# A decoder block with 16 experts: the second pair's gate products moved, three engines in a written order, two small moves in attention

## Chip, cores and metric

The kernel runs on one NeuronCore of one Trainium2 chip. The metric is the device time of one execution in microseconds (us), lower is better; 451.19 us is the median of three runs before the change. The engines are named as in the profile: PE (TensorE, matrix products), DVE (VectorE), ACT (ScalarE), POOL (GpSimd), and SP, which here only issues DMAs.

## What is computed

One block for 256 tokens of 1024 features in float32: two token mixers in parallel, then a mixture of experts. Cut to what matters:

```python
h = rms_norm(x, norm_mix_g)
(f_q, f_k, f_v, f_f, n_q, k_c, v_c, k_s, v_s, k_w, v_w, n_g, g_a, g_b) = split_cols(h @ w_in)
# forgetting attention, 8 heads of 64
out_a = from_heads(fox_attention(rms_norm(f_q), rms_norm(f_k), f_v, log_f)) @ w_fox_up
# sparse attention, 8 query heads over 2 key heads: compressed, selected and window keys
kc = rms_norm(compress_blocks(k_c, cmp_k_w1, cmp_k_w2, cmp_k_pos), nsa_k_g)
vc = compress_blocks(v_c, cmp_v_w1, cmp_v_w2, cmp_v_pos)
out_b = from_heads(nsa_attention(qb, kc, vc, ks_, vs_, kw_, vw_, gates)) @ w_nsa_up
x = x + (sigmoid(g_a) * out_a + sigmoid(g_b) * out_b) @ w_out
# mixture of experts: best of 4 groups, two best of its 4 experts, combine weights w
t = rms_norm(x, norm_ffn_g)
hid = silu(einsum('td,edf->etf', t, w_gate)) * einsum('td,edf->etf', t, w_up)
hid = hid * combine.T[:, :, None]
x = x + einsum('etf,efd->td', hid, w_down)
```

There are 16 experts with a hidden width of 512, so each has 6 MB of weights, 96 MB in all.

## The kernel before

**Attention.** Weight matrices of the mixers are read in pieces of two times 512 columns by 128 rows (`raw`). `hi` makes a rounded copy `wH` on ACT (L173), `lo` the remainder `wL` on DVE (L179); three products per chunk (L199 to L201) then use the high and low parts of weights and activations. The pieces go through a line in which `load`, `hi`, `lo` and `go` (the products of half a piece) run each some pieces apart. `half_a` calls `go`, `lo`, `load` and then the functions it was given; `half_b` calls `go`, `hi` and the functions. All of this is a written order for every engine. Between the pieces stand small jobs: `k_scaled` (L753, two DVE operations) multiplies the keys by their inverse norms into `kdup`, which the PE transposes in `kk_turn` (L730). In a loop over 13 steps n attention units follow: their scores, exponentials, scaling of the scores (`sc`, L579), transposes (L587) and products with the values. A list of background jobs is taken from by `spot`. Three of them are `g_turn`, `c_in` and `c_root`: `c_in` puts the compressed keys and values into one PSUM bank and squares the keys on ACT (L817), `c_root` computes the inverse root on DVE in some ten short operations (from L834) and then reads that bank twice more, for the normalised keys `kcn` (L836) and for `vblk` (L837), the values laid out by head. The bank is one of two with the name `tp`, which go round.

**Experts.** Tokens are routed, and each expert has 64 slots. Experts are taken in pairs, one on each half of the PE's columns, so one product of a pair is two matmuls of 64 columns by 512. Eight pairs follow each other: seven in `expert_pair`, the eighth in `last_pair`. For pair `pr` the PE does `proj` with the gate weights, `proj` with the up weights (each 8 k steps with a matmul per expert, which are 32 rows of the trace, L1347), `scatter` of the previous pair's result to the tokens (L1357, L1358), four transposes of `hid` (L1408) and `down` (L1373). DVE computes `hid` (L1399, written `gh`) from `silu` of the gate product (ACT, L1393 or L1397), and the combine weight of each slot, `csl`; ACT copies the transposes back (L1409). `parts` splits the down product into a high part (ACT, L1361) and a low part (DVE, L1362). `ready` makes the one-hot rows of a pair on DVE (L1007), `slots` turns them into `csl` (PE L1326, DVE L1329 to L1331), and `rows` transposes them for the scatter (PE L1338, DVE L1340); all go through `tp` banks. They are called in the fourth k step of a `proj`: those of pair 0 in its own up products, those of pair 1 in its own gate products (there together with the `rows` of pair 0), all later ones in the up products of the pair before. In odd pairs, between transposes and down products, `gather` collects the tokens of the next two pairs (PE L1317, DVE L1318). After pairs 2 and 4 the residual is added to two accumulators (L1430).

**What sets the order.** In this loop the order of the PE alone is the written one; DVE and ACT are ordered by the scheduler. Expert weights come in tiles of 1 MB, twelve per pair (gate, up, down of two experts, two halves each), issued by SP in that order (L113, at the end L107) into a ring of slots. A load waits until the last matmul that reads the tile before it in its slot has run.

Of the kernel before, what the change touches and what calls it, by code (L numbers as in the profile page):

```python
# [8 lines left out]
F32 = mybir.dt.float32  # L9
# [3 lines left out]
AF = mybir.ActivationFunctionType  # L13
# [17 lines left out]
def block_kernel(ctx, tc, a, out, dbg=None):  # L31
# [608 lines left out]
    with tc.manual_schedule():  # L640
# [128 lines left out]
        half_a(k_scaled)  # L769
# [32 lines left out]
        pw = {}  # L802
# [8 lines left out]
        def c_in():  # L811
            p = pw[0] = bank([128, 512], "tp")
            for f in range(2):
                T.matmul(p[0:32, 0:64], hT[:, f, 0:32], w2[:, 0, f], start=(f == 0), stop=(f == 1))
            for f in range(2):
                T.matmul(p[:, 64:128], hTv[:, f].rearrange("p g r n -> p (g r n)"), w2[:, 1, f], start=(f == 0), stop=(f == 1))
            A.activation(ks_, p[0:32, 0:64], AF.Square, accum_out=kcst[:, 0:1])  # L817

# [12 lines left out]
        ks_ = wk.tile([32, 64], F32, name="kcs", bufs=1)  # L831

        def c_root():
            V.tensor_scalar(kcst[:, 0:1], kcst[:, 0:1], 1.0 / 64, EPS, op0=ALU.mult, op1=ALU.add)  # L834
            rsqrt(kcst[:, 1:2], kcst[:, 0:1], 1, "kc")
            V.tensor_scalar(kcn, pw[0][0:32, None, 0:64].to_broadcast([32, 2, 64]), kcst[:, 1:2], None, op0=ALU.mult)  # L836
            V.tensor_tensor(vblk, pw[0][:, None, 64:128].to_broadcast([128, 8, 64]), hm[:, :, None].to_broadcast([128, 8, 64]), op=ALU.mult)  # L837
# [483 lines left out]
    def slots(pr, Sb):  # L1321

        p = bank([128, 9], "tp")
        for i, cc in enumerate((2 * pr, 2 * pr + 1, 16)):
            for t in range(2):
                T.matmul(p[:, 3 * i:3 * i + 3], Sb[:, t], cb3[:, t, cc], start=(t == 0), stop=(t == 1))  # L1326
        c = wk.tile([128, 3], F32, name="csl")
        j6 = wk.tile([128, 6], F32, name="j6")
        V.tensor_tensor_reduce(j6, p[:, 0:6], half.rearrange("p a b -> p (a b)"), 1.0, 0.0, ALU.mult, ALU.add, c[:, 0:1])  # L1329
        V.tensor_reduce(c[:, 1:2], p[:, 6:9], axis=AX.X, op=ALU.add)  # L1330
        V.tensor_tensor(c[:, 2:3], c[:, 0:1], c[:, 1:2], op=ALU.mult)  # L1331
        return c
# [10 lines left out]
    def proj(w0, w1, xg, o, between=()):  # L1343
        p = bank([128, 512], "z")
        for k in range(8):
# [3 lines left out]
            if k == 3:  # L1349
                for f in between:  # L1350
                    f()
# [34 lines left out]

    def expert_pair(pr, pend):
        xg, o = xgs[pr // 2], pr % 2 * 128
        if pr:
            pg = proj(tiles[2 * pr, 0], tiles[2 * pr + 1, 0], xg, o, pre0)  # L1390
            pre0.clear()
            c, Sb, ST = pre.pop()
            A.activation(sg, pg, AF.Silu, scale=c[:, 1:2])  # L1393
        pu = proj(tiles[2 * pr, 1], tiles[2 * pr + 1, 1], xg, o, [lambda: pre.append(ready(pr + (pr > 0))())])
        if pr == 0:
            c, Sb, ST = pre.pop()
            A.activation(sg, pg0, AF.Silu, scale=c[:, 1:2])  # L1397
# [8 lines left out]
        p = bank([128, 4, 128], "tp")  # L1406
        for f in range(4):
            T.transpose(p[:, f], hid[:, f * 128:f * 128 + 128], ident)  # L1408
        A.activation(hdT, p, AF.Copy)  # L1409
        if pend and pr % 2 == 0:  # L1410
            scatter(*pend, 512, 512)
        if pr % 2 == 1:
            xgs[pr // 2 + 1] = gather(pr // 2 + 1)
        y = rt.tile([128, 2, D], F32R, name="y", tag="yy")
# [16 lines left out]
        if pr == 0:  # L1431
# [3 lines left out]
            pre0.extend([lambda: got.append(rows(Sb)), lambda: pre.append(ready(1)())])  # L1435
# [72 lines left out]
    with tc.manual_schedule(engines={mybir.EngineType.PE}):  # L1508
        pre, pre0 = [], []
        for pr in range(7):  # L1510
            pend = expert_pair(pr, pend)
# [77 lines left out]
```

## Time and profile before

| | |
|---|---|
| runs | 453.54, 451.19, 451.06 us (median 451.19) |
| profiled execution | 451.66 us, of which the span of the trace is 449.7 us |
| PE busy | 430.3 us, 96% |
| DVE, ACT, POOL busy | 214.7, 167.0, 10.5 us |
| granted PE clock, mean | 0.992 |
| DMA | 136.10 MB, mean 303 GB/s |

The profile is of one execution. Times of the trace count from the start of the span. A row of the timeline gives the start, the length, the engine, the line and the instruction (written <- read, the shape, a count); the bracket at its end is the engine's idle time ahead of it and what ended that. A row with a count stands for that many instructions of one kind, one after another. The list of waits sums such idle time by the instruction that waited and the one that ended the wait.

### The profile page before, as it was taken

What the parts mean: (1) busy time and instruction counts of PE and PEld (TensorE: products, weight loads), DVE (VectorE), ACT (ScalarE), POOL (GpSimd) and SP (SyncE); (2) the same over time, 40 slices, a digit from 0 to 9 for tenths busy, and PEclk for the clock granted to TensorE, in tenths of its full rate; (3) what the DMA queues carried; (4) which work ended last, traced back from release to release, by engine and by line L of the source; (5) the groups of instructions that cost most, each with busy time, mean ns of one, the idle gap of its engine ahead of it and who ended that gap; (6) DMA issues with size and microseconds to landing.
All of it is one profiled execution on the core that took longest, in us unless ns stands there. A gap on an engine that the chain in (4) does not pass through costs nothing.

```text
span 449.7 us, 6356 instructions
## 1 busy us (share of the span) xinstructions
PE 430.3 (96%) x2370; PEld 258.9 (58%) x2370; DVE 214.7 (48%) x611; ACT 167.0 (37%) x343; POOL 10.5 (2%) x25
## 2 busy tenths in 40 slices
PE   7998999999999999999999899989999999999994
PEld 4895766767777777878952336333363335433443
DVE  5869776797856565576654224133130512201012
ACT  4786563957767665534732100101011010101011
POOL 8000000000000000000000000000000000000000
PEclk8999999999999999999999999999999999999998
DMA  8699643656763439999889999799999999999922
GB/s 285 131 366 303 216 138 95 222 183 214 254 206 94 129 109 351 408 408 374 352 310 335 351 391 422 280 422 421 420 420 418 420 420 418 422 418 416 391 78 98
DMA packets 41425, 136.10 MB, mean 303 GB/s; under 512 B 7296, under 2 KB 12976, under 8 KB 30384
## 3 DMA queue, kind: packets, MB, share of 16 engines
q1 hardware_dynamic: 41248, 135.54, 80.3%
q8 instruction: 20, 0.33, 0.3%
q10 hardware_dynamic: 144, 0.13, 0.1%
q14 instruction: 13, 0.11, 0.1%
HBM read 134.61 MB, written 1.05 MB: 302 GB/s over the span
## 4 chain that ended last, share of the span: by engine, by line


## 5 line engine op out<-in xcount | busy, mean ns | idle before, releaser
L1347 PE MATMUL z<-m,xg 128*64 128x512 f32 x432 | 100.5, 595 | 0.0
L179 DVE TENSOR_TENSOR wL<-raw,wH 128x1024 fp32r<-128x1024 f32 x48 | 58.4, 1220 | 12.2 <-ACT wH L173 12.0
L173 ACT ACTIVATE wH<-raw 128x1024 fp32r<-128x1024 f32 x48 | 50.5, 1056 | 36.8 <-PE z L201 21.5
L1347 PEld LDWEIGHTS z<-m,xg 128*64 128x64 f32 x432 | 31.5, 137 | 56.5 <-issue 54.6
L199 PE MATMUL z<-wH,hH 128*128 128x512 f32 x128 | 54.4, 425 | 0.0
L200 PE MATMUL z<-wL,hH 128*128 128x512 f32 x128 | 50.4, 393 | 0.0
L201 PE MATMUL z<-wH,hL 128*128 128x512 f32 x128 | 50.3, 393 | 0.0
L1373 PE MATMUL tp<-m,gh 128*64 128x512 f32 (+1 forms) x208 | 49.5, 580 | 0.7 <-ACT gh L1409 0.7
L1373 PEld LDWEIGHTS tp<-m,gh 128*64 128x64 f32 x208 | 15.8, 137 | 28.8 <-issue 25.7
L199 PEld LDWEIGHTS z<-wH,hH 128*128 128x128 f32 x128 | 24.1, 188 | 11.4 <-issue 7.1
L1361 ACT ACTIVATE y<-tp 128x512 fp32r<-128x512 f32 (+1 forms) x15 | 8.6, 583 | 56.7 <-PE tp L1373 56.6
L1340 DVE CAST ST<-tp 128x256 fp32r<-128x256 bf16 x8 | 3.4, 423 | 54.7 <-PE tp L1338 54.7
L1362 DVE TENSOR_TENSOR y<-tp,y 128x512 fp32r<-128x512 f32 (+1 forms) x15 | 10.0, 673 | 36.7 <-ACT y L1361 36.7
L201 PEld LDWEIGHTS z<-wH,hL 128*128 128x128 f32 x128 | 24.1, 188 | 5.5
L1409 ACT ACTIVATE gh<-tp 128x512 f32<-128x512 f32 x7 | 4.2, 598 | 59.6 <-PE tp L1408 59.6
L200 PEld LDWEIGHTS z<-wL,hH 128*128 128x128 f32 x128 | 24.2, 189 | 3.7
L570 ACT ACTIVATE sc<-sc,mx 128x128 f32<-128x128 f32 (+1 forms) x48 | 21.2, 445 | 1.7 <-DVE mx L564 1.4
L1393 ACT ACTIVATE gh<-z,csl 128x512 f32<-128x512 f32 x6 | 4.1, 688 | 39.2 <-PE z L1347 39.2
L1399 DVE SCALAR_TENSOR_TENSOR gh<-gh,csl,z 128x512 f32<-128x512 f32 x7 | 7.9, 1128 | 20.8 <-PE z L1347 15.1
L579 DVE TENSOR_SCALAR sc<-sc,sm 128x128 f32<-128x128 f32 (+1 forms) x48 | 12.1, 316 | 0.4
L1317 PE MATMUL tp<-one,xH 128*128 128x256 f32 x48 | 12.3, 297 | 0.0
L587 PE MATMUL tp<-ident,sc 128*128 128x128 f32 x72 | 10.5, 278 | 1.8 <-DVE vblk L837 1.0
(423 smaller groups left out, 701.5 us busy)
## 6 DMA issues: line engine op xcount, KB each, us to landing
m<-in_w_gate SPq DMA_DIRECT2D x29, 1024.0 KB, 17.2
m<-in_w_up SPq DMA_DIRECT2D x28, 1024.0 KB, 11.5
m<-in_w_down SPq DMA_DIRECT2D x22, 1024.0 KB, 12.5
raw<-in_w_in SPq DMA_DIRECT2D x36, 512.0 KB, 4.6
m<-in_w_down SPq DMA_DIRECT2D x10, 512.0 KB, 9.4
raw<-in_w_out SPq DMA_DIRECT2D x8, 512.0 KB, 10.3
m<-in_cmp_k_w SPq DMA_DIRECT2D x8, 256.0 KB, 8.5
m<-in_cmp_v_w SPq DMA_DIRECT2D x8, 256.0 KB, 4.8
```

The lines of the kernel that those rows point to most:

```text
L173: A.activation(P["H"], P["raw"], AF.Copy)
L179: (eng or V).tensor_tensor(P["L"], P["raw"], P["H"].bitcast(F32), op=ALU.subtract)
L199: T.matmul(p[t], lH[k // 4][:, k % 4, ts], P["H"][:, k - k0], start=(k == 0), stop=False)
L200: T.matmul(p[t], lH[k // 4][:, k % 4, ts], P["L"][:, k - k0], start=False, stop=False)
L201: T.matmul(p[t], lL[k // 4][:, k % 4, ts], P["H"][:, k - k0], start=False, stop=(k == K - 1))
L570: A.activation(sc, sc, AF.Exp, scale=-1.0, bias=u["mx"][:, i, t:t + 1], accum_out=u["sm"][:, i, t:t + 1])
L579: V.tensor_scalar(sc, sc, u["sm"][:, i, t:t + 1], None, op0=ALU.mult)
L587: T.transpose(p[:, 128 * j:128 * j + 128], u["sc"][i][:, 128 * j:128 * j + 128], ident)
L1317: T.matmul(p[:, j], X[t][:, cs], Sr[:, t], start=(i == 0), stop=(i == 3))
L1347: T.matmul(p[64 * i:64 * i + 64], xg[:, k, o + 64 * i:o + 64 * i + 64], w[k // 4][:, k % 4], start=(k == 0), stop=(k == 7), tile_position= ...
L1362: V.tensor_tensor(yHL[:, 1, c0:c0 + n], p[:, 0:n], yHL[:, 0, c0:c0 + n].bitcast(F32), op=ALU.subtract)
L1373: T.matmul(p[64 * i:64 * i + 64, 0:n], hdT[:, f, 64 * i:64 * i + 64], w, start=(f == 0), stop=(f == 3), tile_position=(0, 64 * i))
```

## The change

Four edits. (1) `k_scaled` is issued ahead of the low part of its `half_a`. (2) `c_in` makes `vblk` itself and copies the raw compressed keys to SBUF on ACT (`kcr`), so that `c_root` no longer reads the bank. (3) The gate products of pair 1 are placed ahead of the down products of pair 0, with the transposes of pair 0 in their middle; in pair 1, the transposes of pair 0's one-hot rows, the slots of pair 1 and `silu` stand inside the up products (after the fourth and the sixth k step), and the slots and rows of pair 2 stand between the gather and the down products. `csl` and `j6` get two buffers. (4) The loop's order is the written one on DVE and ACT too.

```diff
@@ half_a(k_scaled)
-        half_a(k_scaled)
+        go()
+        k_scaled()
+        lo()
+        load()
@@ c_in, c_root
-            p = pw[0] = bank([128, 512], "tp")
+            p = bank([128, 512], "tp")
...
             A.activation(ks_, p[0:32, 0:64], AF.Square, accum_out=kcst[:, 0:1])
+            A.activation(kcr, p[0:32, 0:64], AF.Copy)
+            V.tensor_tensor(vblk, p[:, None, 64:128].to_broadcast([128, 8, 64]), hm[:, :, None].to_broadcast([128, 8, 64]), op=ALU.mult)
...
-            V.tensor_scalar(kcn, pw[0][0:32, None, 0:64].to_broadcast([32, 2, 64]), kcst[:, 1:2], None, op0=ALU.mult)
-            V.tensor_tensor(vblk, pw[0][:, None, 64:128].to_broadcast([128, 8, 64]), hm[:, :, None].to_broadcast([128, 8, 64]), op=ALU.mult)
+            V.tensor_scalar(kcn, kcr[:, None, :].to_broadcast([32, 2, 64]), kcst[:, 1:2], None, op0=ALU.mult)
@@ slots
-        c = wk.tile([128, 3], F32, name="csl")
-        j6 = wk.tile([128, 6], F32, name="j6")
+        c = wk.tile([128, 3], F32, name="csl", bufs=2)
+        j6 = wk.tile([128, 6], F32, name="j6", bufs=2)
@@ proj
-    def proj(w0, w1, xg, o, between=()):
+    def proj(w0, w1, xg, o, between=(), after=()):
...
+            if k == 5:
+                for f in after:
+                    f()
@@ expert_pair
-        if pr:
-            pg = proj(tiles[2 * pr, 0], tiles[2 * pr + 1, 0], xg, o, pre0)
-            pre0.clear()
+        if pr == 1:
+
+            pu = proj(tiles[2, 1], tiles[3, 1], xg, o, pre0, [lambda: (pre.append(ready(1)()), silu(pg0[1], pre[0][0])),
+                                                               lambda: later.append(ready(2))])
+            c, Sb, ST = pre.pop(0)
+        elif pr:
+            pg = proj(tiles[2 * pr, 0], tiles[2 * pr + 1, 0], xg, o)
             c, Sb, ST = pre.pop()
-            A.activation(sg, pg, AF.Silu, scale=c[:, 1:2])
-        pu = proj(tiles[2 * pr, 1], tiles[2 * pr + 1, 1], xg, o, [lambda: pre.append(ready(pr + (pr > 0))())])
-        if pr == 0:
+            silu(pg, c)
+            pu = proj(tiles[2 * pr, 1], tiles[2 * pr + 1, 1], xg, o, [lambda: pre.append(ready(pr + 1)())])
+        else:
+            pu = proj(tiles[0, 1], tiles[1, 1], xg, o, [lambda: pre.append(ready(0)())])
             c, Sb, ST = pre.pop()
-            A.activation(sg, pg0, AF.Silu, scale=c[:, 1:2])
+            silu(pg0[0], c)
...
-        p = bank([128, 4, 128], "tp")
-        for f in range(4):
-            T.transpose(p[:, f], hid[:, f * 128:f * 128 + 128], ident)
-        A.activation(hdT, p, AF.Copy)
+
+        def turn():
+            p = bank([128, 4, 128], "tp")
+            for f in range(4):
+                T.transpose(p[:, f], hid[:, f * 128:f * 128 + 128], ident)
+            A.activation(hdT, p, AF.Copy)
+
+        if pr == 0:
+            pg0.append(proj(tiles[2, 0], tiles[3, 0], xg, 128, [turn]))
+        else:
+            turn()
...
+        if later:
+            pre.append(later.pop()())
...
-            pre0.extend([lambda: got.append(rows(Sb)), lambda: pre.append(ready(1)())])
+            pre0.append(lambda: got.append(rows(Sb)))
@@ the loop
-    with tc.manual_schedule(engines={mybir.EngineType.PE}):
+    with tc.manual_schedule(engines={mybir.EngineType.PE, mybir.EngineType.DVE, mybir.EngineType.Activation}):
```

Lines of the new file stand some 4 to 26 further down: L1347 becomes L1351, L1373 L1380, L1399 L1416, L1408 L1427, L1430 L1456.

**PE, from the last up products of pair 0 to its down products.** `z_2670` (`z_2672` after) is the bank of the up products, `z_2761` (`z_2706`) that of pair 1's gate products, read from the tiles `m_2121` and `m_2145` (`m_2123`, `m_2147`, and for the second half `m_2176`, `m_2207`); `m_2077` and `m_2099` are down tiles of pair 0. Each couple of matmuls stands for four. Before:

```order
L1347 MATMUL z_2670<-m_2033,xg 64x512
L1347 MATMUL z_2670<-m_2055,xg 64x512
...
L1408 MATMUL tp_2704<-ident,gh 128x128 x4
L1373 MATMUL tp_2711<-m_2077,gh 64x512
L1373 MATMUL tp_2711<-m_2099,gh 64x512
...
L1347 MATMUL z_2761<-m_2121,xg 64x512
```

and after:

```order
L1351 MATMUL z_2672<-m_2035,xg 64x512
L1351 MATMUL z_2672<-m_2057,xg 64x512
...
L1351 MATMUL z_2706<-m_2123,xg 64x512
L1351 MATMUL z_2706<-m_2147,xg 64x512
...
L1427 MATMUL tp_2715<-ident,gh 128x128 x4
L1351 MATMUL z_2706<-m_2176,xg 64x512
L1351 MATMUL z_2706<-m_2207,xg 64x512
...
L1380 MATMUL tp_2730<-m_2079,gh 64x512
L1380 MATMUL tp_2730<-m_2101,gh 64x512
```

The transposes now have half of pair 1's gate products ahead of them and half behind, and the down products follow.

**DVE, pair 2.** `one_` are one-hot rows, `j` and `csl` the two reductions of the slots' bank, `gh` is `hid`, `y` the low part of the down product; `o_` and `s_` are accumulators to which the residual `xH`, `xL` is added. Before:

```order
L1340 CAST ST<-tp_2989 128x256
L1007 TENSOR_TENSOR one_3095<-slot,rank__2607 128x128 x2
L1399 SCALAR_TENSOR_TENSOR gh<-gh,csl,z_2965 128x128x4
L1430 TENSOR_TENSOR o_2663<-o_2663,xH_2221 128x512
L1329 ISA j_2985,csl<-tp_2977,half 128x6
L1329 ISA csl 128x1
L1330 TENSOR_REDUCE csl<-tp_2977 128x1
L1430 TENSOR_TENSOR o_2663<-o_2663,xL_2222 128x512
L1331 TENSOR_TENSOR csl<-csl 128x1
```

and after:

```order
L1333 ISA j_2987,csl<-tp_2979,half 128x6
L1333 ISA csl 128x1
L1334 TENSOR_REDUCE csl<-tp_2979 128x1
L1335 TENSOR_TENSOR csl<-csl 128x1
L1344 CAST ST<-tp_2991 128x256
L1416 SCALAR_TENSOR_TENSOR gh<-gh,csl,z_2967 128x128x4
L1369 TENSOR_TENSOR y<-tp_3020,y 128x512
L1369 TENSOR_TENSOR y<-tp_3031,y 128x512
L1456 TENSOR_TENSOR o_2665<-o_2665,xH_2223 128x512
```

The reductions stand ahead of `hid`, and the residual behind the low parts of the down product.

**DVE, the compressed keys and values.** `tp_859` (`tp_860` after) is the bank of `c_in`, `sc` are scores, `sm` their scale, `kcst` the squared norms, `rs_u` steps of the inverse root. Before:

```order
L579 TENSOR_SCALAR sc<-sc,sm 128x256
L834 TENSOR_SCALAR kcst<-kcst 32x1
L120 TENSOR_SCALAR kcst<-kcst 32x1
...
L124 SCALAR_TENSOR_TENSOR kcst<-rs_u,kcst 32x1
L836 TENSOR_SCALAR kcn<-tp_859,kcst 32x128
L837 TENSOR_TENSOR vblk<-tp_859,hm 128x512
L179 TENSOR_TENSOR wL<-raw,wH 128x1024
```

and after:

```order
L821 TENSOR_TENSOR vblk<-tp_860,hm 128x512
L573 RECIPROCAL sm<-sm 128x4
L575 TENSOR_TENSOR sm<-sm,ngate 128x4
L579 TENSOR_SCALAR sc<-sc,sm 128x128
...
L839 TENSOR_SCALAR kcst<-kcst 32x1
...
L841 TENSOR_SCALAR kcn<-kcr,kcst 32x128
L179 TENSOR_TENSOR wL<-raw,wH 128x1024
```

`vblk` moved from behind the inverse root to ahead of the scaling of the scores, and `kcn` reads `kcr` instead of the bank.

## Rows read from the trace of the kernel before

**Rows 1.** the page, part 1: busy time, share and instructions of each engine
```profile
PE 430.3 (96%) x2370; PEld 258.9 (58%) x2370; DVE 214.7 (48%) x611; ACT 167.0 (37%) x343; POOL 10.5 (2%) x25
```

**Rows 2.** windows: length, then busy us by engine, PEclk, DMA share, GB/s
```profile
20.00:420.00 400.00, 390.23 (x2149) 233.84 (x2148) 197.29 (x545) 150.05 (x306) 0.61 (x1) 1.00 0.84 317
80.00:100.00 20.00, 19.60 (x109) 14.20 (x108) 17.14 (x62) 14.22 (x37) 0.00 (x0) 1.00 0.60 205
429.00:432.00 3.00, 2.73 (x24) 1.49 (x20) 0.96 (x2) 0.17 (x1) 0.00 (x0) 1.00 0.20 72
```

**Rows 3.** waits of PE in the whole span: us in total, times, longest
```profile
PE tp L1408 <- DVE csl L1330: 2.4, 3, 1.3
...
PE tp L587 <- DVE sc L579: 0.8, 2, 0.4
```

**Rows 4.** timeline, 36.5 to 43.5 us: start, length, engine, line, instruction
```profile
40.37 1.22 DVE L179 TENSOR_TENSOR wL<-raw,wH 128x1024 fp32r<-128x1024 f32 x1
...
41.50 1.29 DVE L753 TENSOR_TENSOR m<-kraw,krs 128x512 f32<-128x512 f32 x2
...
42.84 0.66 PE L730 MATMUL tp<-ident,m 128*128 128x128 f32 x4 [1.16 <-DVE m L753]
```

**Rows 5.** timeline, 62 to 68.2 us
```profile
63.19 0.18 DVE L573 RECIPROCAL sm<-sm 128x4 f32<-128x4 f32 x1 [0.45 <-ACT sc L570]
...
63.61 1.01 DVE L579 TENSOR_SCALAR sc<-sc,sm 128x128 f32<-128x128 f32 x4
63.63 0.20 ACT L817 ACTIVATE kcs<-tp 32x64 f32<-32x64 f32 x1
...
66.13 0.49 PE L587 MATMUL tp<-ident,sc 128*128 128x128 f32 x3
...
66.85 0.67 DVE L837 TENSOR_TENSOR vblk<-tp,hm 128x512 f32<-128x512 f32 x1
...
67.67 0.52 PE L587 MATMUL tp<-ident,sc 128*128 128x128 f32 x3 [1.05 <-DVE vblk L837]
```

**Rows 6.** timeline of pair 0, 242 to 250 us
```profile
246.75 1.08 DVE L1399 SCALAR_TENSOR_TENSOR gh<-gh,csl,z 128x512 f32<-128x512 f32 x1 [3.25 <-PE z L1347]
...
247.89 0.66 PE L1408 MATMUL tp<-ident,gh 128*128 128x128 f32 x4 [1.28 <-DVE gh L1399]
...
249.23 1.08 PE L1373 MATMUL tp<-m,gh 128*64 128x512 f32 x4 [0.69 <-ACT gh L1409]
```

**Rows 7.** timeline of pair 1, 255 to 280 us, in three stretches
```profile
256.15 3.60 PE L1347 MATMUL z<-m,xg 128*64 128x512 f32 x16
...
260.69 0.48 PE L1326 MATMUL tp<-cb,one 128*128 128x3 bf16 x6 [0.72 <-DVE one L1007]
...
268.25 0.31 PE L1326 MATMUL tp<-cb,one 128*128 128x3 bf16 x6
...
278.65 0.64 PE L1373 MATMUL tp<-m,gh 128*64 128x512 f32 x1
...
278.75 0.69 DVE L1318 TENSOR_TENSOR xg<-tp,g_row 128x512 f32<-128x512 f32 x1 [0.32 <-PE tp L1317]
```

**Rows 8.** timeline of pair 2, 299 to 303.5 us
```profile
300.12 1.13 DVE L1399 SCALAR_TENSOR_TENSOR gh<-gh,csl,z 128x512 f32<-128x512 f32 x1 [2.85 <-issue]
...
302.07 0.16 DVE L1330 TENSOR_REDUCE csl<-tp 128x1 f32<-128x3 f32 x1
...
302.38 0.63 PE L1408 MATMUL tp<-ident,gh 128*128 128x128 f32 x4 [1.27 <-DVE csl L1330]
```

**Rows 9.** timeline of the SP queue: issues of two loads
```profile
190.93 0.46 SPq L113 DMA_DIRECT2D m<-in_w_gate  x1
...
254.63 0.80 SPq L113 DMA_DIRECT2D m<-in_w_up  x2
```

**Rows 10.** waits of the SP queue, 226 to 300 us
```profile
SPq L113 <- PE tp L1373: 18.9, 3, 10.9
```

**Rows 11.** timeline of the last pair, 427 to 449.7 us
```profile
432.63 4.08 PE L1373 MATMUL z<-m,gh 128*64 128x512 f32 x18
```

More of the change, by code (lines that the diff above doesn't have):

```diff
@@ L801, in block_kernel @@
         hTv = at.tile([128, 2, 2, 4, 16], F32, name="hTv")
-        pw = {}
         def g_turn():
@@ L831, in block_kernel @@
         ks_ = wk.tile([32, 64], F32, name="kcs", bufs=1)
+        kcr = wk.tile([32, 64], F32, name="kcr", bufs=1)
         def c_root():
@@ L1385, in ready, with silu @@
         return rest_
+    def silu(pg, c):
+        A.activation(sg, pg, AF.Silu, scale=c[:, 1:2])
+    pg0, later = [pg0], []
     def expert_pair(pr, pend):
         xg, o = xgs[pr // 2], pr % 2 * 128
-        if pr:
-            pg = proj(tiles[2 * pr, 0], tiles[2 * pr + 1, 0], xg, o, pre0)
-            pre0.clear()
+        if pr == 1:
[4 more added lines that the diff above has]
+            pg = proj(tiles[2 * pr, 0], tiles[2 * pr + 1, 0], xg, o)
             c, Sb, ST = pre.pop()
-            A.activation(sg, pg, AF.Silu, scale=c[:, 1:2])
-        pu = proj(tiles[2 * pr, 1], tiles[2 * pr + 1, 1], xg, o, [lambda: pre.append(ready(pr + (pr > 0))())])
-        if pr == 0:
+            silu(pg, c)
+            pu = proj(tiles[2 * pr, 1], tiles[2 * pr + 1, 1], xg, o, [lambda: pre.append(ready(pr + 1)())])
+        else:
+            pu = proj(tiles[0, 1], tiles[1, 1], xg, o, [lambda: pre.append(ready(0)())])
             c, Sb, ST = pre.pop()
-            A.activation(sg, pg0, AF.Silu, scale=c[:, 1:2])
+            silu(pg0[0], c)
         fours = lambda h: h.rearrange("p (q k) -> p q k", k=4)
```

## Prediction

> **What bounds the kernel now.** I read the engine lines of the page first. TensorE is busy for 430.3 us, 96% of the span, twice as much as any other engine [rows 1]. The windows come next: over the 400 us from 20 to 420 us TensorE is busy 390.23 us and its granted clock is 1.00, the upper of its two levels (2.4 GHz) [rows 2]. So the matmuls run at full speed nearly all the time, and no edit that keeps their number can save anything but TensorE's gaps. The DMA share over the same stretch is 0.84, so the stream of weights is the second thing to watch.
>
> Then I read the waits of TensorE, because they list the gaps. The largest entry of the experts' loop is its transposes of `hid` waiting for VectorE's `csl`, 2.4 us in three places [rows 3]. The timeline shows the gaps one by one [rows 4 to 8]. The span is 449.7 us and the profiled execution 451.66 us. I work in differences, which apply to either.
>
> **The change part by part.** The number of matmuls stays. Beside moves, only one small ScalarE copy is added. Five places are touched.
>
> *(a) Keys scaled ahead of the low part.* TensorE stands 1.16 us in front of the transposes at 42.84 us, because VectorE first makes a low weight part (40.37 us, 1.22 us long) and only then the scaled keys (41.50 us, 1.29 us for both) [rows 4]. With the two in the other order the scaled keys start at 40.37, end at 41.66, and the transposes can start some 0.1 us later, at 41.75 instead of 42.84: 1.1 us saved. What is late next is the low part, by 1.3 us; its piece of weights is multiplied several halves of a chunk later, and six matmuls of each half lie between, which covers it. The ends are -1.16 (no wait at all) and 0 (the next user of that low part waits as long); I take **-1.1**, the value worked from the rows.
>
> *(b) `vblk` early.* TensorE waits 1.05 us at 67.67 us. Its second group of score transposes needs the PSUM bank that `vblk` still reads at 66.85 us, 0.67 us long, and that read stands behind a chain of short VectorE operations [rows 5]. In the new code `vblk` is made as soon as the bank is written and ScalarE has taken its two small reads: the square at 63.63 us of 0.20 us, and the added copy, priced like it at 0.20. `vblk` then runs from about 64.1 to 64.8 and the bank is free 2.7 us earlier. In exchange the scaling of the scores, at 63.61 us and 1.01 us long [rows 5], moves behind `vblk`: after two small operations on the sums (they began at 63.19, so 0.42 us) its first half ends near 65.7 and its second near 66.2. TensorE needs the first half at 66.13 and the second about 0.5 us later, so it has 0.4 us in hand each time. Ends: -1.05 if the scaling keeps that margin, 0 if it is late by what it gains. I take **-0.9**.
> Here a rule bears on the order. VectorE's `vblk` and ScalarE's square read different columns of one bank, and the new order lets `vblk` wait for ScalarE. The Trainium skill, "PSUM — Partial Sum Buffer", section "PSUM bank collisions raise a hardware error", states that two engines may not touch the same bank and quadrant of partitions at one time, reads included; by that rule the wait is compulsory and the added copy delays `vblk` by its own length. Without the rule `vblk` could start at 63.5 and the part would be worth -1.05 outright; with it the margin is 0.4 us, hence -0.9. No run here shows what an overlap would do.
>
> *(c) Pair 0: gate products of pair 1 in front of its down products.* Before, nothing stands between the last up product and the transposes: TensorE waits 1.28 us for `hid` (VectorE, 246.75, 1.08 us) and 0.69 us for the copy of the transposed `hid` [rows 6]. After, half of a pair's gate products stand there: half a set took 3.60 us at 256.15 [rows 7], which hides 1.28 us, and the other half hides the copy that ScalarE makes of the transposes. Nothing is added, since these products stood behind the down products before. So 1.28 + 0.69 = **-2.0**. Needed for that: the gate tiles of pair 1. The load of the last of them was issued at 190.93 us [rows 9], 55 us before. The ends are -2.2 (the transposes also lie closer together) and 0 (products wait for something I don't see).
>
> *(d) Pair 1.* The wait of 0.72 us for the one-hot rows at 260.69 [rows 7] goes, since four products now stand between `rows(0)` and the slots: -0.7. New: slots and rows of pair 2 are put between gather and down products. The gather's last bank is freed by a VectorE multiply that starts at 278.75 and takes 0.69 us [rows 7]. The rows of pair 2 need that bank, free at 279.44, and the down products need the slots' bank, free once VectorE, busy until 279.44, has done two short reductions, at about 279.7. So down products start at 279.8 instead of 278.65: 1.15 us later, less what slots and rows themselves took inside the up products, where they leave: 0.31 us for the slots' six products at 268.25 and a little for the rows, some 0.35. That is +0.8. Queued behind that wait are only the down products. Sum **+0.1**, with ends -0.7 (no new wait) and +0.8.
>
> *(e) Pairs 2, 4, 6.* The transposes wait 1.27 us at 302.38 for `csl`. `hid` ended at 301.25 already, but a residual add follows it on VectorE, and the reduction that frees the transposes' bank came only behind that, at 302.07 for 0.16 us [rows 8]. In the new order the reductions stand before `hid` and the adds behind the parts of the down products, so `hid` alone decides: transposes at 301.31 instead of 302.38, -1.07. At pairs 4 and 6 the same entry holds the rest of the 2.4 us [rows 3], 1.1 us; of each I let the 0.2 us stay that `hid` itself asks for at pair 2 (1.27 less 1.07): -0.35 twice. Sum **-1.8**. Ends: -2.4 and 0 (something else held behind in the written order). The adds, four per pair, then lie beside down products and the next gate products, where VectorE has nothing else that TensorE waits for.
>
> Costed at nothing: `csl` and `j6` in two buffers; the gathers' one-hots behind `hid` (in odd pairs eight scatter products and the transposes lie beside both; without that cover I price it like the wait at 260.69, 0.7 us per odd pair); the written order of ScalarE, whose instructions in the loop follow each other as they did.
>
> *The queue of weight loads.* Its order stays, but a load waits until its slot is free. The slot of pair 0's first down tile came free before the load at 254.63 [rows 9]. Now a set of gate products comes first (two halves of 3.4 to 3.6 us, say 6.9) and waits of 2.0 go, so it is free about 4.9 us later, near 259.5. Further on, SP had one wait of 10.9 us on a down product [rows 10], a time in which nothing new was asked for; the loads held back catch up there, so I expect the stream's end to move by a few tenths only. At the end of the kernel the DMA share is down to 0.20 from 429 to 432 us, while 18 of the last pair's down products begin only at 432.63 [rows 2, 11]: some slack is left. Cost nothing, price of the lost cover in the rival below.
>
> Sum: -1.1 - 0.9 - 2.0 + 0.1 - 1.8 = -5.7. The profiled execution would go from 451.66 to 445.96; it lies 0.47 above the median of the runs, 451.19, so on the median **445.5 us**.
>
> **The rivals.**
> *Attention gives it back.* Parts (a) and (b) bring TensorE forward by 2.0 us in a stage where VectorE is nearly as busy: 17.14 of 20 us from 80 to 100 us, and TensorE waits twice for the scaled scores there [rows 2, 3]. If VectorE bounds that stretch, TensorE meets later waits of the same size and only (c) to (e) count: 451.2 - 3.7 = 447.5. For it: those two waits, 0.8 us. Against: VectorE also loses its idle time around 41 and 67 us, so it comes forward with TensorE.
> *The reordered pairs gain nothing.* In the loop (c) is undone by a wait at pair 1 (`hid` there stands behind `silu`, which now comes only at the sixth k step) and (d) costs its upper end: 451.2 - 1.1 - 0.9 - 1.8 + 0.8 = 448.2. For it: the new wait at the gather is sure to exist. Against: eight scatter products stand between `hid` and the transposes of pair 1.
> *The change doesn't do what it says*: the waits stay with another releaser, 450 to 451.
> *Slower: the weight stream becomes the bound.* If the 4.9 us by which the first down slot comes free later are not caught up in SP's wait of 10.9 us, every later load lands 4.9 us late; from the point where the slack at the end is used up, the last pair waits for its tiles and the end moves with them: 451.2 + 4.9 - 2.0 (only the attention parts, ahead of all this, remain) = 454.1. For it: a DMA share of 0.84 over 400 us [rows 2]. Against: the 10.9 us, and the share of 0.20 before the last down products.
>
> **How the numbers follow.** A measurement here tells a change of about 1%, 4.5 us, so faster means under 446.7. Forecast 0.62; attention gives it back 0.19; the pairs gain nothing 0.09; no effect 0.04; slower 0.06. The forecast's own spread from the ends of (a) to (e) is some -1.6 and +1.5 us, which leaves 0.07 of its 0.62 above 446.7; of the second case 0.05 lies under it. Faster 0.60, same 0.34, slower 0.06. The range goes from 443.9 (445.5 less 1.6) up over the second and third case to 448.6.
>
> **What would show it.** In the new profile the waits of TensorE should have no entry for the scaled keys, for `vblk`, for `csl` or for `hid` in pair 0; a new one should stand between gather and down products of pair 1, about 1 us. The first load of the up tiles after pair 0 should be issued near 257.5 (259.5 less the 2.0 of attention). The prediction is wrong if the waits on the scaled scores (0.8 us) grow by over 1 us, if the last pair waits for a DMA, or if TensorE's busy time differs from 430.3 by more than a few tenths.

## The result and the profile after

| | before | after |
|---|---|---|
| median of the runs | 451.88 us (451.06 to 453.54, 4 runs) | 445.2 us (444.87 to 446.2, 4 runs) |
| profiled execution, span | 451.66, 449.7 us | 444.87, 442.8 us |
| ratio | | 0.9851, 95% interval 0.9816 to 0.9887 |

The change takes 1.5% off, 6.7 us by the ratio. The forecast was 445.5 us. TensorE's busy time went from 430.3 [rows 1] to 429.1 us, and 0.9 of these 1.2 us fell ahead of everything that was changed (33.07 us busy up to 36.36 us before, 32.20 up to 35.36 after). So the gain is in its gaps. Part 1 of the page after:

```profile
PE 429.1 (97%) x2370; PEld 257.5 (58%) x2370; DVE 214.4 (48%) x611; ACT 167.0 (38%) x344; POOL 10.5 (2%) x25
```

The windows after, with the columns of [rows 2]. Over the same 400 us TensorE is now busy 395.77 instead of 390.23 us at the same clock. VectorE is no busier than before in the stretch from 80 to 100 us, which now holds work that lay some 3 us later:

```profile
20.00:420.00 400.00, 395.77 (x2188) 236.14 (x2188) 195.89 (x538) 150.17 (x307) 0.61 (x1) 1.00 0.84 319
80.00:100.00 20.00, 19.60 (x112) 14.33 (x110) 16.39 (x58) 14.24 (x34) 0.00 (x0) 1.00 0.68 222
```

The waits of TensorE after. Of [rows 3] the entry for `csl`, the longest of the loop, is gone; the scaled scores (L579) stay as they were. In the loop one is new, 0.6 us on the gather's multiply (L1322), and 0.6 us in three places remains on `hid` (L1416). The first line stands ahead of the loop and was 1.1 us before too; the last one, at the output weights, was 0.2 us:

```profile
PE s L1217 <- DVE one L1011: 1.1, 1, 1.1
...
PE tp L587 <- DVE sc L579: 0.7, 2, 0.4
PE tp L1342 <- DVE xg L1322: 0.6, 1, 0.6
PE tp L1427 <- DVE gh L1416: 0.6, 3, 0.2
...
PE z L1095 <- ACT wH L173: 0.5, 1, 0.5
```

Where the time went is read by taking the same matmul in both traces and subtracting its starts. The lead is worked from starts to the nanosecond, so its last digit can differ by one from that of the two columns:

| matmul | before | after | lead | gained since the line above | forecast |
|---|---|---|---|---|---|
| L693, last one ahead of the first edit | 36.36 | 35.36 | 1.00 | 1.00, not by the change | 0 |
| L730, transposes of the scaled keys | 42.84 | 40.77 | 2.08 | 1.08 (a) | 1.1 |
| L587, second group of score transposes | 67.67 | 64.43 | 3.23 | 1.15 (b) | 0.9 |
| L1347, up products of pair 0 | 242.96 | 240.02 | 2.94 | -0.29 | 0 |
| L1373, down products of pair 1 | 278.65 | 273.32 | 5.32 | 2.38 (c, d) | 1.9 |
| L1408, transposes of pair 2 | 302.38 | 295.99 | 6.39 | 1.07 (e) | 1.07 |
| end of the span | 449.7 | 442.8 | 6.9 | 0.5 (e, pairs 4 and 6, less 0.1 at the end) | 0.7 |

The first microsecond of lead arises before anything that was changed: the profiled execution before had a mean granted clock of 0.89 in its first 15 us, the one after 1.00. So the traces show 5.9 us for the change, and the medians 6.7. The loss of 0.29 us lies at the products with the output weights. The experiments look for the rest.

The places one by one. In (a) the keys now stand ahead of the low part, and TensorE follows 0.06 us behind them, against [rows 4]:

```profile
39.42 1.29 DVE L753 TENSOR_TENSOR m<-kraw,krs 128x512 f32<-128x512 f32 x2
...
40.63 1.22 DVE L179 TENSOR_TENSOR wL<-raw,wH 128x1024 fp32r<-128x1024 f32 x1
...
40.77 0.66 PE L730 MATMUL tp<-ident,m 128*128 128x128 f32 x4
```

In (b) `vblk` runs at 62.04 us, behind ScalarE's square and copy, and all six score transposes follow each other; in [rows 5] three of them waited 1.05 us:

```profile
61.61 0.20 ACT L819 ACTIVATE kcs<-tp 32x64 f32<-32x64 f32 x1
...
61.81 0.20 ACT L820 ACTIVATE kcr<-tp 32x64 f32<-32x64 f32 x1
...
62.04 0.69 DVE L821 TENSOR_TENSOR vblk<-tp,hm 128x512 f32<-128x512 f32 x1 [1.32 <-ACT kcr L820]
...
63.05 1.00 DVE L579 TENSOR_SCALAR sc<-sc,sm 128x128 f32<-128x128 f32 x4
...
64.11 0.82 PE L587 MATMUL tp<-ident,sc 128*128 128x128 f32 x6
```

The bracket at `vblk` names ScalarE's copy. The Trainium skill, "PSUM — Partial Sum Buffer", section "PSUM bank collisions raise a hardware error", asks for that wait between two engines that read one bank in the same quadrant of partitions, and the trace has it; it cost nothing, since the scaled scores were ready in time.

In pair 0 the two waits of [rows 6] are gone: `hid` and ScalarE's copy of the transposes run beside pair 1's gate products.

```profile
244.16 1.11 DVE L1416 SCALAR_TENSOR_TENSOR gh<-gh,csl,z 128x512 f32<-128x512 f32 x1 [3.60 <-DMA m<-in_w_gate]
...
247.03 0.66 PE L1427 MATMUL tp<-ident,gh 128*128 128x128 f32 x4
...
247.62 3.65 PE L1351 MATMUL z<-m,xg 128*64 128x512 f32 x16
247.73 0.60 ACT L1428 ACTIVATE gh<-tp 128x512 f32<-128x512 f32 x1 [6.59 <-PE tp L1427]
...
251.10 1.46 PE L1380 MATMUL tp<-m,gh 128*64 128x512 f32 x6
```

In pair 1 the new wait is there: the rows of pair 2 wait 0.63 us for the gather's last multiply, and the down products, which need the bank that VectorE reduces at 273.06, start right behind ([rows 7] has the old order).

```profile
272.38 0.69 DVE L1322 TENSOR_TENSOR xg<-tp,g_row 128x512 f32<-128x512 f32 x1 [0.32 <-PE tp L1321]
...
273.06 0.15 DVE L1334 TENSOR_REDUCE csl<-tp 128x1 f32<-128x3 f32 x1
273.12 0.27 PE L1342 MATMUL tp<-identb,one 128*128 128x128 bf16 x2 [0.63 <-DVE xg L1322]
...
273.32 0.64 PE L1380 MATMUL tp<-m,gh 128*64 128x512 f32 x1
```

In pair 2 the transposes wait 0.20 us, for `hid` alone, instead of 1.27 [rows 8]:

```profile
294.81 1.12 DVE L1416 SCALAR_TENSOR_TENSOR gh<-gh,csl,z 128x512 f32<-128x512 f32 x1 [3.05 <-PE z L1351]
...
295.99 0.66 PE L1427 MATMUL tp<-ident,gh 128*128 128x128 f32 x4 [0.20 <-DVE gh L1416]
```

The loads of weights: the first load behind pair 0's down products is issued at 256.45 us, 1.8 us later than in [rows 9] although TensorE is 2.9 us ahead there, and the longest wait of the queue is 11.9 us, against 10.9 in [rows 10].

```profile
256.45 1.28 SPq L113 DMA_DIRECT2D m<-in_w_up  x3
```

```profile
SPq L113 <- PE tp L1380: 24.4, 3, 11.9
```

### The profile page after: what moved, and what is told of

The parts are those of the page before. It is cut to its first block, busy times and chain, and to the rows that moved or that the text cites. A ratio compares the mean times of both kernels' runs of the same rounds, so it can differ in the third digit from the quotient of the medians.

```text
span 442.8 us, 6352 instructions
## 1 busy us (share of the span) xinstructions
PE 429.1 (97%) x2370; PEld 257.5 (58%) x2370; DVE 214.4 (48%) x611; ACT 167.0 (38%) x344; POOL 10.5 (2%) x25
## 3 DMA queue, kind: packets, MB, share of 16 engines
HBM read 134.61 MB, written 1.05 MB: 306 GB/s over the span
## 4 chain that ended last, share of the span: by engine, by line
## 5 line engine op out<-in xcount | busy, mean ns | idle before, releaser
L1351 PE MATMUL z<-m,xg 128*64 128x512 f32 x432 | 100.7, 594 | 0.0
L1351 PEld LDWEIGHTS z<-m,xg 128*64 128x64 f32 x432 | 31.4, 137 | 56.1 <-issue 54.0
L1380 PE MATMUL tp<-m,gh 128*64 128x512 f32 (+1 forms) x208 | 49.4, 579 | 0.0
L1380 PEld LDWEIGHTS tp<-m,gh 128*64 128x64 f32 x208 | 15.8, 137 | 28.4 <-issue 26.0
L1333 DVE CUSTOM_DVE_ANT_0 j<-tp,half 128x6 f32<-128x6 f32 x8 | 1.3, 164 | 40.3 <-PE tp L1330 40.3
L1416 DVE SCALAR_TENSOR_TENSOR gh<-gh,csl,z 128x512 f32<-128x512 f32 x7 | 7.9, 1131 | 19.7 <-PE z L1351 15.2
L579 DVE TENSOR_SCALAR sc<-sc,sm 128x128 f32<-128x128 f32 (+1 forms) x48 | 12.1, 316 | 0.4
L1322 DVE TENSOR_TENSOR xg<-tp,g_row 128x512 f32<-128x512 f32 x12 | 8.3, 692 | 7.6 <-PE tp L1321 7.6
```

The lines of the kernel that those rows point to most:

```text
L579: V.tensor_scalar(sc, sc, u["sm"][:, i, t:t + 1], None, op0=ALU.mult)
L1351: T.matmul(p[64 * i:64 * i + 64], xg[:, k, o + 64 * i:o + 64 * i + 64], w[k // 4][:, k % 4], start=(k == 0), stop=(k == 7), tile_position= ...
L1380: T.matmul(p[64 * i:64 * i + 64, 0:n], hdT[:, f, 64 * i:64 * i + 64], w, start=(f == 0), stop=(f == 3), tile_position=(0, 64 * i))
```

## The experiments

Each ran beside the kernel before on the same chip, whose medians were 452.05, 452.14 and 451.9 us for the three groups of four. Effects under 1 us are below what one interval resolves, so for those the starts of the same matmul are compared as above, with the lead that arises ahead of the first edit taken off.

### Only the second buffers

```diff
-        c = wk.tile([128, 3], F32, name="csl")
-        j6 = wk.tile([128, 6], F32, name="j6")
+        c = wk.tile([128, 3], F32, name="csl", bufs=2)
+        j6 = wk.tile([128, 6], F32, name="j6", bufs=2)
```

> The kernel before with a second buffer for csl and j6 and nothing else; the order of VectorE and ScalarE stays the scheduler's. Theory of the prediction (the written order of VectorE removes the waits of pairs 2, 4 and 6): no gain, 0.0 us, the 2.4 us of waits on csl stay. Rival (with one buffer the next csl cannot be written before hid has read the old one, so no order could place it ahead; the buffer alone does it): those waits fall from 2.4 to about 0.6 us, now on hid, and the time falls by 1.8 us, ratio 0.996.

Measured: 450.47 us, ratio 0.9962 (0.9945 to 0.9979). The wait on `csl` is gone with these two words; what remains at pairs 2, 4 and 6 is 0.2 us each, on `hid`, and pair 0's 1.3. By the starts of the same matmuls, pairs 2, 4 and 6 gain 1.0, 0.3 and 0.3 us:

```profile
PE tp L1408 <- DVE gh L1399: 1.8, 4, 1.3
```

The scheduler itself put the reductions ahead of `hid` once it could. With one buffer the next pair's `csl` may not be written before `hid` has read this pair's, so it stood behind `hid` because it had to. This profile also caught something else, in pair 0. The window of the two waits and the one right behind them:

```profile
246.00:248.80 2.80, 1.15 (x8) 0.63 (x10) 0.91 (x1) 0.60 (x1) 0.00 (x0) 1.00 1.03 394
249.50:252.00 2.50, 2.50 (x8) 0.72 (x6) 0.00 (x0) 0.00 (x0) 0.00 (x0) 0.50 1.01 419
```

and the timeline there:

```profile
246.96 0.66 PE L1408 MATMUL tp<-ident,gh 128*128 128x128 f32 x4 [1.28 <-DVE gh L1399]
...
248.31 3.18 PE L1373 MATMUL tp<-m,gh 128*64 128x512 f32 x8 [0.69 <-ACT gh L1409]
...
256.92 3.60 PE L1347 MATMUL z<-m,xg 128*64 128x512 f32 x16
```

The granted clock was still 1.00 in the stretch of the waits. Right behind them it is 0.50, the lower level of 1.2 GHz, and eight rows of down products take 3.18 us. That costs 1.70 us: TensorE is 0.93 us ahead of the kernel before at the transposes (246.96 us) and 0.77 us behind it at pair 1's gate products (256.92, against 256.15 in [rows 7]). It is taken up below.

### Part a alone

```diff
-        half_a(k_scaled)
+        go()
+        k_scaled()
+        lo()
+        load()
```

> The kernel before with only the keys scaled ahead of the low part. Theory: the transposes start right behind the products, their wait of 1.16 us goes, TensorE is 1.1 us ahead of the kernel before from there on to the end of attention, and the time falls by 1.1 us (ratio 0.9976). Rival (attention gives it back where VectorE is busy): ahead by 1.1 us at 43 us, but by under 0.3 us at the end of attention, time the same.

Measured: 451.38 us, ratio 0.9991 (0.9973 to 1.001): no change that can be told, though the interval reaches to the 1.1 us of the forecast. Locally the part did what was forecast, a lead of 1.08 us at the key transposes. In the profiled execution all of it was lost between 197 and 208 us, in the product with the output weights. There TensorE waits 0.8 us for a high part and 0.5 us for a low part (0.2 us before):

```profile
PE z L1094 <- ACT wH L173: 0.8, 1, 0.8
...
PE s L1095 <- DVE wL L179: 0.5, 1, 0.5
```

The high part waited 0.46 us for the DMA of its piece:

```profile
196.33 1.06 ACT L173 ACTIVATE wH<-raw 128x1024 fp32r<-128x1024 f32 x1 [0.46 <-DMA raw<-in_w_out]
...
197.44 0.50 PE L1094 MATMUL z<-wH,mixH 128*128 128x512 f32 x1 [0.81 <-ACT wH L173]
```

So attention can give a gain back, as the rival said, but in this profile it does so at the pieces of the output weights, not where VectorE is busy. Whether the other runs lost it in the same place is not known.

### The changed kernel without part a

```diff
-        go()
-        k_scaled()
-        lo()
-        load()
+        half_a(k_scaled)
```

> The changed kernel with part a alone undone (keys scaled behind the low part again). Theory of the prediction: 1.1 us slower than the changed kernel, 446.5, with the wait of 1.16 us on the scaled keys back. Rival (attention gives it back, as a_only showed when the pieces of the output weights came late): TensorE is 1.1 us behind at 43 us but by under 0.4 us at the end of that stage, and the time is that of the changed kernel within 0.4 us.

Measured: 446.18 us (445.65 to 448.43), ratio 0.9875 (0.9851 to 0.9899), beside 445.2 and 445.4 us for the two measurements of the changed kernel: 0.8 to 1.0 us slower, and 1.1 to 1.3 us by the ratios, which allow for the other chip. Its wait on the keys is back at 1.2 us, and it has only 0.2 us of waiting at the output weights, where the changed kernel has 0.5 to 0.7. The wait at the output weights doesn't follow from part a, though: three kernels below that have parts a and b (TensorE's order alone, and the two with pair 2's slots moved) show 0.2 us there too, and their traces lose nothing. So part a seems to be worth most of its 1.1 us in the changed kernel, but the intervals of the two overlap. Why its profile alone lost everything stays open: both have the same pieces in the same order, and in that profile the high part waited for a landing.

This profile is of the slowest of its five runs, 2.8 us above the fastest, and its start shows a reason. The granted clock is at the lower level from 8 to 14.5 us, and TensorE is 1.6 us behind the kernel before at 36 us, where the changed kernel was 1.0 ahead:

```profile
8.00:14.50 6.50, 6.14 (x17) 4.55 (x18) 5.53 (x21) 4.64 (x12) 2.61 (x4) 0.50 1.08 360
```

Four other profiles, of kernels with and without the change (the one before among them), have 3 us at 0.50 between 8 and 12 us. So runs of any of these kernels can differ by clock that is lost at the start.

### Part b alone

```diff
+            A.activation(kcr, p[0:32, 0:64], AF.Copy)
+            V.tensor_tensor(vblk, p[:, None, 64:128].to_broadcast([128, 8, 64]), hm[:, :, None].to_broadcast([128, 8, 64]), op=ALU.mult)
...
-            V.tensor_scalar(kcn, pw[0][0:32, None, 0:64].to_broadcast([32, 2, 64]), kcst[:, 1:2], None, op0=ALU.mult)
-            V.tensor_tensor(vblk, pw[0][:, None, 64:128].to_broadcast([128, 8, 64]), hm[:, :, None].to_broadcast([128, 8, 64]), op=ALU.mult)
+            V.tensor_scalar(kcn, kcr[:, None, :].to_broadcast([32, 2, 64]), kcst[:, 1:2], None, op0=ALU.mult)
```

> The kernel before with only the early vblk and the copied keys. Theory: the wait of 1.05 us on vblk goes, TensorE is 0.9 to 1.1 us ahead from there to the end of attention, the two waits on the scaled scores stay at 0.8 us together, and the time falls by 1.0 us (ratio 0.998). Rival (attention gives it back): the waits on the scaled scores grow to 1.5 us or more, time the same.

Measured: 450.64 us, ratio 0.9971 (0.9953 to 0.9989), 1.3 us. The lead over the kernel before grows by some 1.1 us up to the second group of score transposes and is kept to the end of the span; the waits on the scaled scores are 0.7 us together. The theory holds, the rival does not.

### The loop alone

```diff
+        half_a(k_scaled)
-        go()
-        k_scaled()
-        lo()
-        load()
...
+            V.tensor_tensor(vblk, pw[0][:, None, 64:128].to_broadcast([128, 8, 64]), hm[:, :, None].to_broadcast([128, 8, 64]), op=ALU.mult)
```

(parts a and b undone in the changed kernel)

> The changed kernel with attention as it was before (parts a and b undone). Theory of the prediction: parts c, d and e give 3.7 us (ratio 0.9918) whatever attention does, with the new wait of 1 us behind the gather of pair 1. Rival (the stream of weights limits what the loop gains): under 3 us, and a wait of TensorE on a DMA in the last two pairs.

Measured: 447.27 us (446.71 to 448.08), ratio 0.9892 (0.9871 to 0.9914): 4.9 us, more than the 3.7 forecast. In the traces the lead grows by 4.1 us. No wait on a DMA appears; the two waits of attention and the new one at the gather do:

```profile
PE tp L730 <- DVE m L753: 1.2, 1, 1.2
...
PE tp L587 <- DVE vblk L837: 1.1, 1, 1.1
...
PE tp L1338 <- DVE xg L1318: 0.6, 1, 0.6
```

### The changed kernel again, and pairs 0 and 1 as they were

> The changed kernel once more, as the yardstick for the three others on this chip. Theory: 6.2 to 6.9 us under the kernel before, ratio about 0.986. Rival (the first comparison, of four runs each, flattered it): 4.5 us or less, ratio above 0.990.

Measured: 445.4 us (444.73 to 445.5), ratio 0.9847 (0.9827 to 0.9867). The first result repeats.

In the next kernel `expert_pair` is the old one for pairs 0 and 1; the other edits stay:

```diff
-        if pr == 0:
-            pg0.append(proj(tiles[2, 0], tiles[3, 0], xg, 128, [turn]))
-        else:
-            turn()
+        p = bank([128, 4, 128], "tp")
+        for f in range(4):
+            T.transpose(p[:, f], hid[:, f * 128:f * 128 + 128], ident)
+        A.activation(hdT, p, AF.Copy)
...
-        if later:
-            pre.append(later.pop()())
```

> The changed kernel with pairs 0 and 1 as they were before (parts c and d undone; a, b, the second buffers and the written order stay). Theory of the prediction: 1.9 to 2.3 us slower than the changed kernel, with waits of 1.3 and 0.7 us in pair 0 and 0.7 us in pair 1. Addition (an idle stretch of some 2 us in pair 0 lets TensorE's granted clock fall to its lower level in part of the executions, as the profile of two_bufs showed): 2.5 to 4 us slower in the median, runs spread over 2 us or more, and a mean granted clock of 0.991 to 0.994 in the slower runs against 0.995 or more for the changed kernel.

Measured: 449.05 us, ratio 0.9925 (0.9899 to 0.9951), 3.65 us slower than the changed kernel. The seven runs spread from 447.26 to 450.5 us. The two fastest, 447.26 and 447.49, have a mean granted clock of 0.998; the three slowest, 449.68 to 450.5, have 0.990 or 0.991. The five runs of the changed kernel beside it lie within 0.8 us. So about 2 us is lost even in the fastest runs, and up to 3 us more in others.

The profile, in which the clock stays at 1.00 in pair 0, accounts for 2.8 of the 3.65 us. From the up products of pair 0 to the down products of pair 1 this kernel falls 0.4 us behind the kernel before, where the changed kernel gains 2.4 on it. The 0.4 us is a cost of its own: `hid` starts 0.50 us after the up products end, against 0.14 before (products from 242.96 us for 3.65, `hid` at 246.75 [rows 6]), and the wait in pair 0 is 1.63 instead of 1.28 us:

```profile
241.06 3.65 PE L1351 MATMUL z<-m,xg 128*64 128x512 f32 x16
...
245.21 1.08 DVE L1403 SCALAR_TENSOR_TENSOR gh<-gh,csl,z 128x512 f32<-128x512 f32 x1 [3.60 <-PE z L1351]
...
246.35 0.66 PE L1412 MATMUL tp<-ident,gh 128*128 128x128 f32 x4 [1.63 <-DVE gh L1403]
```

What delays `hid` there stays open. Some 0.9 us is left for the clock. The mean clocks don't say where it was lost: the slowest run of the kernel without part a has 0.991 too, with its loss at the start.

### The waits of pair 0 filled

The kernel is the one just told, run again as a yardstick, and once with products that nothing reads in its two waits:

```diff
+        def busy(n):
+            for i in range(n if pr == 0 else 0):
+                T.matmul(acc[0][0][:, 0:256], identb, warmer, start=True, stop=True, skip_group_check=True)
+
+        busy(10)
         p = bank([128, 4, 128], "tp")
         for f in range(4):
             T.transpose(p[:, f], hid[:, f * 128:f * 128 + 128], ident)
         A.activation(hdT, p, AF.Copy)
+        busy(5)
```

> no_pair_move once more, as the yardstick for pair0_busy on this chip. Both theories: median near 449, runs between 447 and 451.

> no_pair_move with 15 small bf16 products, whose result nothing reads, in pair 0: ten in front of the transposes and five behind them, which fit into the waits of 1.3 and 0.7 us. Theory (the idle of pair 0 lets TensorE's granted clock fall in part of the executions, and that is the part of c that the sum did not hold): the waits are filled, their length stays, yet the median falls from 449 to about 447.5 and the runs lie within 1.5 us of each other, with clocks of 0.994 or more. Rival (the scatter of no_pair_move has another origin): median and scatter as no_pair_move, or slower by what the products take over the waits.

Measured: 449.5 us (447.9 to 450.38) for the yardstick, 447.83 us (447.32 to 448.97) with the products. The work is larger and the down products start no earlier (in both profiles 6.63 us after the last half of the up products begins), yet the median falls by 1.7 us, the spread from 2.5 to 1.65 us, and the lowest clock of a run rises from 0.988 to 0.994. Its timeline in pair 0: the products end before `hid` does, so 0.44 us of waiting stays, and the eight rows of down products take 1.94 us, against the 3.18 us above. The yardstick's profile has 1.94 us too, so the two profiles don't differ in clock there; the runs do.

```profile
243.24 1.26 PE L1412 MATMUL o<-warmer,identb 128*128 128x256 bf16 x10
...
244.95 0.66 PE L1417 MATMUL tp<-ident,gh 128*128 128x128 f32 x4 [0.44 <-DVE gh L1403]
...
245.44 0.71 PE L1412 MATMUL o<-warmer,identb 128*128 128x256 bf16 x5
...
246.29 1.94 PE L1377 MATMUL tp<-m,gh 128*64 128x512 f32 x8
```

That supports the idle of pair 0 as a place where the clock is lost: clock that goes at the start should be lost in both kernels alike. But these are seven and six runs, and the intervals of the two ratios (0.9922 to 0.9964, 0.9893 to 0.9936) overlap a little. It is shown directly in one profile (the one above with the window at 0.50); the other five profiles with pair 0 in its old order have 1.00 there, and for the other long runs only the mean clock is known.

### The order of TensorE alone

```diff
-    with tc.manual_schedule(engines={mybir.EngineType.PE, mybir.EngineType.DVE, mybir.EngineType.Activation}):
+    with tc.manual_schedule(engines={mybir.EngineType.PE}):
```

> The changed kernel with the written order for TensorE alone, VectorE and ScalarE left to the scheduler; the second buffers stay. Theory that two_bufs supports (the buffers, not the written order, remove the waits on csl): same time as the changed kernel within 0.3 us, no wait on csl at pairs 2, 4 and 6. Rival (the written order matters): 1.0 to 1.8 us slower with such waits.

Measured: 445.19 us (444.34 to 445.49), ratio 0.9841 (0.982 to 0.9862), the changed kernel within 0.2 us. No wait on `csl` is left. The written order for VectorE and ScalarE, the part that the change is named for, gives nothing that can be measured.

### Slots of pair 2 in pair 2's gate products

```diff
-        if later:
-            pre.append(later.pop()())
...
-            pg = proj(tiles[2 * pr, 0], tiles[2 * pr + 1, 0], xg, o)
+            pg = proj(tiles[2 * pr, 0], tiles[2 * pr + 1, 0], xg, o, [lambda: pre.append(later.pop()())] if later else ())
```

> The changed kernel with slots and rows of pair 2 moved from between gather and down products of pair 1 into pair 2's own gate products, after their fourth k step. Theory: the wait of 0.63 us behind the gather and the late down bank go, 0.7 us less than the changed kernel (the insertion of some 0.37 us stays), ratio to before about 0.0015 lower. Rival (a new wait in the gate products of pair 2, for banks that the down product's parts hold): same as the changed kernel.

Measured: 444.88 us (444.65 to 445.36), ratio 0.9837 (0.9816 to 0.9857), 0.5 us under the changed kernel beside it, which the intervals don't tell apart. The wait behind the gather is gone and none took its place: from the scatter in pair 1 to the one in pair 3, TensorE gains 0.47 us on the kernel before, where the changed kernel loses 0.02.

### The same, and two banks for the last transposes

```diff
-        p = bank([128, 4, 128], "tp")
         for h in range(2):
-            for f in (2 * h, 2 * h + 1):
-                T.transpose(p[:, f], hid[:, f * 128:f * 128 + 128], ident)
-            A.activation(hdT[:, 2 * h:2 * h + 2], p[:, 2 * h:2 * h + 2], AF.Copy)
+            p = bank([128, 2, 128], "tp")
+            for j in range(2):
+                f = 2 * h + j
+                T.transpose(p[:, j], hid[:, f * 128:f * 128 + 128], ident)
+            A.activation(hdT[:, 2 * h:2 * h + 2], p, AF.Copy)
```

> slots2_in_gate, and in the last pair each half of the transposes gets a PSUM bank of its own, so that the second half no longer waits for ScalarE's copy of the first. Theory: the wait of 0.53 us there shrinks to about 0.2 us, the end comes 0.3 us earlier than in slots2_in_gate, 0.8 us earlier than the changed kernel. Rival (the second half then waits as long for the second half of hid, and the first down products were the bound): the same as slots2_in_gate.

Measured: 444.15 us (443.77 to 445.26), ratio 0.9835 (0.9812 to 0.9857), the lowest median of all, 1.1 to 1.3 us under the changed kernel, and 0.5 to 0.7 us by the ratios, which allow for the other chip; the intervals overlap. The wait of 0.53 us in the last pair is down to 0.2, now on `hid`:

```profile
PE tp L1490 <- DVE gh L1485: 0.2, 1, 0.2
```

In the timeline the second half of the transposes no longer stands behind ScalarE's copy of the first (424.45 us, 0.38 us long) but runs beside it:

```profile
424.45 0.38 ACT L1491 ACTIVATE gh<-tp 128x256 f32<-128x256 f32 x1 [6.64 <-PE tp L1490]
...
424.57 0.44 PE L1490 MATMUL tp<-ident,gh 128*128 128x128 f32 x2 [0.22 <-DVE gh L1485]
```

## Why the prediction was right

The time, the direction and the size held: 445.5 us forecast, 445.2 measured. By its steps:

- **(a), -1.1**: 1.08 us in the trace. The step that left out something is its "what is late next": the low part was late without harm, as said, but 0.3 us of the lead of (a) and (b) was given back at the output weights, and the profile of part a alone lost all of it there. Three other profiles with both parts gave nothing back, so this is no fixed cost. The rival "attention gives it back" had the effect in small and the wrong place.
- **(b), -0.9**: 1.15 us in the trace, 1.3 in the median of the part alone. The margin of 0.4 us for the scaled scores was enough, so the cautious end was not needed.
- **(c), -2.0, and (d), +0.1**: together 2.4 us in the trace against 1.9. Split at the first up product of pair 1, (c) gave some 2.2 and (d) gained some 0.2 instead of losing 0.1. The new wait of (d) came as worked out: the rows wait for the gather's multiply and the down products for the reduction, which start 1.05 us later behind the gather than before (1.15 forecast). The wait that goes in pair 1 and both of pair 0 went, and no wait on `hid` came in pair 1, so the rival on the reordered pairs fell. In the median the kernel with pairs 0 and 1 in their old order is 3.65 us slower, of which its own later `hid` is 0.4. Some 0.9 us more than the traces show is left. (c) priced the idle of pair 0 at its length; in part of the executions it can also cost clock, 1.70 us in the one profile that caught it, and the one profile of before did not show that. How often it happens isn't known.
- **(e), -1.8**: 1.7 us. The size is right and the reason wrong. The prediction gave it to the new order and cost the second buffers at nothing; the buffers alone do it, and the written order adds nothing to them. The written order with one buffer was not tried.
- **The queue of loads**: the first load came at 256.45 us against 257.5 forecast, of which 1.0 is the start of this execution. No wait of TensorE on a DMA appears, in this kernel or in the two faster ones, so the rival on the weight stream fell. The slack it spoke of did shrink, though. From 429 to 432 us the DMA share was 0.20 [rows 2]; the same work now lies at 422 to 425 us, and the share there is 1.05, since the stream came forward less than TensorE did. How much slack is left was not tried.

```profile
422.00:425.00 3.00, 2.72 (x24) 1.49 (x20) 0.96 (x2) 0.18 (x1) 0.00 (x0) 1.00 1.05 387
```

- **The signs of being wrong**: the waits on the scaled scores did not grow and no tile came late. The third sign, a busy time of TensorE that differs by more than a few tenths, did come: 1.2 us less. It says little about the change, since 0.9 of it lies ahead of the first edit, where the clock of the profile before was 0.89; the prediction had not allowed for that.

The sum of the forecast, 5.7 us, agrees with the 5.9 us that the traces give to the change, and in part that is luck: (b), (c) and (d) gave 0.75 us more than forecast, the output weights and pairs 4 and 6 some 0.5 less. That the time itself was met within 0.3 us is luck too: the change is 6.7 us by the ratio, 1.0 more than forecast, and the median that the forecast started from, 451.19 us, lay 0.7 below the one measured here. What the medians have beyond the traces, 0.8 us, fits clock that pair 0 no longer loses, but the runs don't separate that from clock lost at the start.

## What to carry to other kernels

When an engine does things in an awkward order, look first at the buffers: a tile with one buffer fixes the order of its writer behind the last reader, and a second buffer is a change of two words. An idle stretch of an engine whose clock can fall can cost more than its length, and one profile need not show it: look at several runs and, in every profile at hand, at the granted clock stretch by stretch, since a run's mean clock doesn't say where it was lost. A gain early in a kernel can be lost at the next place that waits for a transfer, so a part is to be judged by the lead at the end of its stage.

## What the runs showed that was not expected

A busy kernel can lose TensorE's clock over short waits: behind 1.28 us of idle, 0.66 us of transposes and 0.69 us of idle, the granted clock was 0.50 in one execution (eight rows of down products in 3.18 instead of 1.94 us, 1.70 us lost in all) and 1.00 in five others with such waits. Fifteen products of no use in these waits took 1.7 us off the median.
